# A float32 transformer trunk on one core: the first pair of hidden chunks of each half step by eight plain block products of 512 columns

## The chip, the cores and the metric

The program runs on one core of a Trainium2 chip. The time is the device time of one execution in microseconds (us); lower is better. A core has TensorE (PE in the profile; its weight loads are PEld), VectorE (DVE), ScalarE (ACT), GpSimd (POOL) and SyncE (SP, here the issuer of the weight DMAs). Each engine takes its instructions from a list of its own, in the order of that list, and waits at an instruction until what it needs is there.

## The reference

Two layers on 512 tokens of width 1024, in float32. Each layer has two half steps (a gated feed-forward net of hidden width 2816), a token mixer between them and a gated embedding at the end:

```python
def rms_norm(x, g, eps=NORM_EPS):
    x32 = x.astype(f32)
    y = x32 * lax.rsqrt(jnp.mean(x32 * x32, axis=-1, keepdims=True) + eps)
    return (y * g.astype(f32)).astype(x.dtype)

def swiglu(h, wg, wu, wd):
    return (jax.nn.silu(h @ wg) * (h @ wu)) @ wd
...
    for i in range(DEPTH):
        h = h + 0.5 * swiglu(rms_norm(h, norm_ffn_a[i]), ffn_a_wg[i], ffn_a_wu[i], ffn_a_wd[i])
        hn = rms_norm(h, norm_mix[i])
        ...
        h = h + mix
        h = h + 0.5 * swiglu(rms_norm(h, norm_ffn_b[i]), ffn_b_wg[i], ffn_b_wu[i], ffn_b_wd[i])
        gate = jax.nn.sigmoid(rms_norm(h, norm_ple[i]) @ ple_gate[i])
        h = h + gate * (p[i] @ ple_proj[i])
    return rms_norm(h, final_norm)
```

The mixers are left out here; the change does not touch them.

## The kernel before

The state is kept transposed: `hT[c]` holds 128 of the 1024 channels (c = 0 to 7) for all 512 tokens. A float32 factor is split into a high part (rounded to fp32r, a copy on ACT) and a low part (the rest, a subtraction on DVE), and a product is three matmuls: high by high, high by low, low by high (`mm3`). The normalization is not applied to the operand. Only the gain is; the reciprocal root mean square R of each token is worked out from the running sum of squares `acc` by `norm_stats` (four matmuls `ssum`, eleven tiny DVE instructions, a diagonal matrix L336, a matmul `rbc` that spreads it over the partitions, a copy L345 into `Rt`) and multiplied in after the product.

A half step (`ffn`) runs through 22 hidden chunks of 128 in sections of 4, 6, 6 and 6 (`SECTIONS`). Chunks are taken in pairs j (`dq`, `pair`): for a pair, gate and up projection are 1024 by 512 by 512 products, cut into a two by two scheme (channel blocks in even and odd c, tokens in two halves of 256, the two chunks) and done by **seven** block products instead of eight. Each `product` is 24 matmuls of 256 columns (2 for gate and up, 4 channel blocks, 3 for the split). The seven need sums of weights, which `split_next` adds up on DVE (L165) before it splits them (L174 on ACT, L176 on DVE), seven pieces for a pair; and sums of operands, `xr`, seven combinations of the activations. `right(i)` makes those of channels 2i and 2i+1: two scalings on ACT (L366, L368), four sums of 256 columns on DVE (L377 to L380), and the split of seven blocks (L373 on ACT, L374 on DVE, in parts of 3 and 4). Op 0 is needed by the first product (tile X), op 3 by the second (tile Y), and both need all four i. Between the pairs stand the down projections of the section before (`down`, 512 columns each).

There are four half-step starts. In the two of `fa` in layer 0 (the launch) and of `fb` in both layers, `prep` calls `right` after every second channel block becomes final: at the launch after a transposition (L440), in `fb` after the last output projection of the mixer (`out_proj`, the add L772). In `fa` of layer 1 it happens inside the gated embedding `ple` (L553 to L556), where `prep(..., part=True)` makes most of the sums, and `rest` (L386 to L390) the two blocks that `ple` does not leave free; `ple_x` is the operand of `ple`.

The order of the instructions on each engine is set at build time by a scheduler that plays the program through; the program's order gives priority. Weights come through six raw buffers (`load_next`) into five split slots (`hl`); a slot is free again when the product that reads it is done (`used`, `pump`). Each of the PSUM tags A (X), B (Y) and C (Z) has two banks.

Of the kernel before, what the change touches and what calls it, by code (L numbers as in the profile page):

```python
# [18 lines left out]
P = 128  # L19
# [19 lines left out]
def trunk(ctx, tc, a, stop=None):  # L39
# [7 lines left out]
    def bank(tag, name="ps"):  # L47
        return psum.tile([P, NT], F32, tag=tag, name=name)
# [172 lines left out]
    def plan_ffn(wg, wu, wd):  # L221


        base = [sum(SECTIONS[:s]) for s in range(len(SECTIONS))]
        steps = []

        def dq(j):
            q = {}
            for f, par in ((0, 0), (1, 0), (1, 1), (0, 1)):
                cs = slice((2 * j + f) * P, (2 * j + f + 1) * P)  # L230
                dmas = [(lambda t, u=u: t.rearrange("p (i n) -> p i n", i=4)[:, :, u * P : (u + 1) * P],
                         w[:, cs].rearrange("(i two p) n -> p two i n", two=2, p=P)[:, par])
                        for u, w in enumerate((wg, wu))]
                q[f, par] = Raw(1024, dmas, True)
            a, b, c, d = q[0, 0], q[0, 1], q[1, 0], q[1, 1]
            steps.append(("dq", j, [
                Piece(1024, a), Piece(1024, None, (0, c, d)), Piece(1024, None, (0, 0, a)),
                Piece(1024, None, (0, 0, b)), Piece(1024, None, (1, a, c)), Piece(1024, b),
                Piece(1024, d)]))

        def dn(s, u):
            n = SECTIONS[s]
            rows = slice(base[s] * P, (base[s] + n) * P)
            steps.append(("dn", s, u, Unit(n, 256, [(0, n, 0, wd[rows, u * 256 : (u + 1) * 256])], True)))

        for s, n in enumerate(SECTIONS):
            us = list(range(4)) if s else []
            js = [base[s] // 2 + k for k in range(n // 2)]
            for k, j in enumerate(js):
                dq(j)  # L250
                for _ in range(len(us) // (len(js) - k)):
                    dn(s - 1, us.pop(0))
        for u in range(4):
            dn(len(SECTIONS) - 1, u)
        return steps
# [88 lines left out]
        else:  # L344
            nc.vector.tensor_copy(dst, ps)  # L345

    def prep(c, l, which, sq=True, eng=nc.vector, part=False):


        g = gains[:, l, which, c : c + 1]  # L350
        if which % 2:
            h, lw = ple_x[c] if which == 3 else (xh[c], xl[c])
            nc.scalar.activation(h, hT[c], AF.Copy, scale=g)
            nc.vector.scalar_tensor_tensor(lw, hT[c], g, h.bitcast(F32),
                                           op0=ALU.mult, op1=ALU.subtract)
        elif c % 2:
            right(c // 2, l, which, part)
        if sq:
            squares(c, eng)

    ple_x = [(hid[4 + 2 * c], hid[5 + 2 * c]) for c in range(4)]
    ple_x += [tuple(xrt[:, s, 1024 + c * NT : 1536 + c * NT] for s in range(2)) for c in range(4)]

    def right(i, l, which, part=False):
# [6 lines left out]
        def halve(o, v, n):  # L371
            h, lw, s = xr[:, 0, o : o + n, i, :], xr[:, 1, o : o + n, i, :], V[:, v : v + n]
            nc.scalar.activation(h, s, AF.Copy)  # L373
            nc.vector.tensor_tensor(lw, s, h.bitcast(F32), op=ALU.subtract)  # L374
# [9 lines left out]
    def rest(i, l, which):  # L384

        g = gains[:, l, which, 2 * i + 1 : 2 * i + 2]  # L386
        h, lw = (xr[:, s, 1:3, i, :] for s in range(2))
        x = hT[2 * i + 1].rearrange("p (o n) -> p o n", o=2)
        nc.scalar.activation(h, x, AF.Copy, scale=g)
        nc.vector.scalar_tensor_tensor(lw, x, g, h.bitcast(F32), op0=ALU.mult, op1=ALU.subtract)  # L390

    def squares(c, eng=nc.vector):
        if c == 0:
# [51 lines left out]
    pump()  # L445


    def ffn(steps, nxt, side=None):

        state = {}  # L450

        def pair(j, ps, first):
            X, Y, Z = bank("A", "X"), bank("B", "Y"), bank("C", "Z")
            k = [0]

# [88 lines left out]
    def ple(pt, ids, R, nxt):  # L544

        for c in range(KD):
            pg, pj = bank("A", "pg"), bank("B", "pj")
            for k in range(2):
                mm3(pj, *ids[c].w(8 + k), *pt[k], k == 0, k == 1)
            for k in range(KD):  # L550
                mm3(pg, *ids[c].w(k), *ple_x[k], k == 0, k == KD - 1)
            s = sc("sg")
            nc.vector.tensor_tensor(s, pg, R, op=ALU.mult)  # L553
            nc.scalar.activation(s, s, AF.Sigmoid)
            nc.vector.tensor_tensor(s, pj, s, op=ALU.mult)
            nc.vector.tensor_tensor(hT[c], s, hT[c], op=ALU.add)  # L556
            done(ids[c])
            prep(c, *nxt, part=True)
        for i in range(4):
            rest(i, *nxt)  # L560

    def last_ple(pt, d, rcol):

# [12 lines left out]
        for i, iu in enumerate(d["pg"]):  # L576
            for b in range(NB):
                ts_ = slice(b * P, (b + 1) * P)
                ps = bank("A", "pg")
                for k in range(KD):  # L580
                    mm3(ps, ple_x[k][0][:, ts_], ple_x[k][1][:, ts_], *iu[k // 4].w(k % 4),
                        k == 0, k == KD - 1)
                ph = bank("D", "hps")
                for c in range(4):
# [482 lines left out]


    for l, d in enumerate(plans):
        ffn(d["fa"], (l, 1))  # L1070
        rcol, _ = norm_stats(False)
        (odd_mixer if l else even_mixer)(d, rcol, (l, 2))
        box = []
        ffn(d["fb"], (l, 3), lambda: box.append(load_p(l)))
# [44 lines left out]
```

## Time and profile before

| | |
|---|---|
| three runs | 2177.76, 2178.45, 2184.96 us; median 2178.45 us |
| profiled execution, its own time | 2182.95 us |
| its span | 2181.2 us |
| PE busy | 2059.2 us (94%), 13283 matmuls |
| DVE busy | 1696.4 us (78%) |
| ACT busy | 1068.1 us (49%) |
| POOL busy | 281.1 us (13%) |
| mean granted clock of TensorE | 0.966 |
| DMA | 190.06 MB, mean 87 GB/s |

The span is that of one profiled execution, cut by its own clock; the few us between span and time lie around it. PE's share is an average. In nearly all of the 40 slices of the page PE is busy for nine tenths or more; the first slice and the few at the starts of half steps are not, and there the granted clock is lower too (0.6 in the first slice). So what a change at a half-step start is worth is read from the stretch from the first final channel block to the point from which PE runs without a gap.

### The profile page before, as it was taken

What the parts mean: (1) busy time and instruction counts of PE and PEld (TensorE: products, weight loads), DVE (VectorE), ACT (ScalarE), POOL (GpSimd) and SP (SyncE); (2) the same over time, 40 slices, a digit from 0 to 9 for tenths busy, and PEclk for the clock granted to TensorE, in tenths of its full rate; (3) what the DMA queues carried; (4) which work ended last, traced back from release to release, by engine and by line L of the source; (5) the groups of instructions that cost most, each with busy time, mean ns of one, the idle gap of its engine ahead of it and who ended that gap; (6) DMA issues with size and microseconds to landing.
All of it is one profiled execution on the core that took longest, in us unless ns stands there. A gap on an engine that the chain in (4) does not pass through costs nothing.

```text
span 2181.2 us, 34325 instructions
## 1 busy us (share of the span) xinstructions
PE 2059.2 (94%) x13283; PEld 1885.6 (86%) x13283; DVE 1696.4 (78%) x2682; ACT 1068.1 (49%) x1722; POOL 281.1 (13%) x249
## 2 busy tenths in 40 slices
PE   4999999999788899999999999999999879999998
PEld 3999998988766799999779999989989769999986
DVE  7888777688988897786788877767656689877775
ACT  4544444355555554444555444445655555444443
POOL 2000000433411000000410000014323110000011
PEclk6999999998899899999999999999999979999999
DMA  4333333321111233333333333222212214333331
GB/s 130 107 110 96 92 97 100 78 61 48 60 39 39 73 102 107 112 105 93 86 90 107 102 102 116 88 80 78 69 44 75 78 39 122 98 95 103 114 109 39
DMA packets 302051, 190.06 MB, mean 87 GB/s; under 512 B 14208, under 2 KB 292800, under 8 KB 301888
## 3 DMA queue, kind: packets, MB, share of 16 engines
q1 hardware_dynamic: 298592, 184.36, 28.6%
q10 hardware_dynamic: 2912, 2.46, 0.4%
q8 instruction: 104, 1.70, 0.3%
q0 software_dynamic: 384, 1.05, 0.2%
q14 instruction: 59, 0.48, 0.1%
HBM read 185.73 MB, written 2.10 MB: 86 GB/s over the span
## 4 chain that ended last, share of the span: by engine, by line
PE 84%; DVE 12%; issue 1%; ACT 1%; DMA 1%; SPq 0%; POOL 0%; DVEq 0%; ACTq 0%; POOLq 0%
PE X L464 22%; PE Y L464 11%; PE down L310 7%; PE down L309 7%; PE down L308 7%; PE Z L464 6%; PE proj L308 3%; PE proj L309 3%; PE proj L310 3%; DVE fr L165 1%; DVE xr L374 1%; PE outp L309 1%; PE outp L308 1%; PE outp L310 1%; PE pt L717 1%
## 5 line engine op out<-in xcount | busy, mean ns | idle before, releaser
L174 ACT ACTIVATE hl<-fr 128x1024 fp32r<-128x1024 f32 (+5 forms) x620 | 522.2, 860 | 662.2 <-PE X L464 285.0
L176 DVE TENSOR_TENSOR hl<-fr,hl 128x1024 fp32r<-128x1024 f32 (+2 forms) x485 | 548.0, 1137 | 155.8 <-ACT hl L174 150.2
L464 PE MATMUL X<-xr,hl 128*128 128x256 f32 x4224 | 539.5, 284 | 27.4 <-DVE xr L374 24.5
L464 PEld LDWEIGHTS X<-xr,hl 128*128 128x128 f32 x4224 | 522.4, 191 | 39.4 <-DVE xr L374 28.6
L464 PE MATMUL Y<-xr,hl 128*128 128x256 f32 x2112 | 274.2, 285 | 19.8 <-ACT xr L373 11.2
L464 PEld LDWEIGHTS Y<-xr,hl 128*128 128x128 f32 x2112 | 259.9, 191 | 26.5 <-ACT xr L373 12.5
L310 PE MATMUL down<-hid,hl 128*128 128x512 f32 x704 | 274.2, 390 | 0.0
L308 PE MATMUL down<-hid,hl 128*128 128x512 f32 x704 | 274.2, 390 | 0.0
L309 PE MATMUL down<-hid,hl 128*128 128x512 f32 x704 | 274.2, 389 | 0.0
L165 DVE TENSOR_TENSOR fr<-fr 128x1024 f32<-128x1024 f32 x176 | 218.6, 1242 | 24.7 <-DMA fr<-in_ffn_b_wu_dram 11.5
L176 POOL TENSOR_TENSOR hl<-fr,hl 128x512 fp32r<-128x512 f32 (+3 forms) x135 | 155.8, 1172 | 271.5 <-ACT hl L174 205.8
L308 PE MATMUL proj<-hl,xr 128*128 128x384 f32 (+2 forms) x512 | 170.4, 336 | 5.4 <-DVE fr L633 4.1
L309 PE MATMUL proj<-hl,xr 128*128 128x384 f32 (+2 forms) x512 | 170.2, 333 | 0.0
L310 PE MATMUL proj<-hl,xr 128*128 128x384 f32 (+2 forms) x512 | 169.7, 333 | 0.0
L310 PEld LDWEIGHTS down<-hid,hl 128*128 128x128 f32 x704 | 132.2, 188 | 26.3
L308 PEld LDWEIGHTS down<-hid,hl 128*128 128x128 f32 x704 | 132.2, 188 | 25.1
L309 PEld LDWEIGHTS down<-hid,hl 128*128 128x128 f32 x704 | 132.2, 188 | 24.6
L464 PE MATMUL Z<-xr,hl 128*128 128x256 f32 x1056 | 147.9, 284 | 2.7 <-DVE hl L176 1.7
L464 PEld LDWEIGHTS Z<-xr,hl 128*128 128x128 f32 x1056 | 135.3, 192 | 3.1 <-DVE hl L176 1.9
L641 POOL TENSOR_TENSOR fr<-fr 128x512 f32<-128x512 f32 (+1 forms) x72 | 90.6, 1265 | 219.2 <-DVE fr L633 109.8
L308 PEld LDWEIGHTS proj<-hl,xr 128*128 128x128 f32 x512 | 98.0, 192 | 7.4 <-DVE fr L633 4.3
L513 DVE TENSOR_TENSOR fr<-down,fr 128x512 f32<-128x512 f32 x128 | 87.6, 684 | 20.3 <-PE down L310 19.4
(211 smaller groups left out, 2920.3 us busy)
## 6 DMA issues: line engine op xcount, KB each, us to landing
fr<-in_ffn_a_wg_dram SPq DMA_DIRECT2D x88, 256.0 KB, 2.9
fr<-in_ffn_a_wu_dram SPq DMA_DIRECT2D x88, 256.0 KB, 3.3
fr<-in_ffn_b_wg_dram SPq DMA_DIRECT2D x88, 256.0 KB, 2.9
fr<-in_ffn_b_wu_dram SPq DMA_DIRECT2D x88, 256.0 KB, 3.3
fr<-in_ffn_a_wd_dram SPq DMA_DIRECT2D x48, 384.0 KB, 3.7
fr<-in_ffn_b_wd_dram SPq DMA_DIRECT2D x48, 384.0 KB, 3.8
fr<-in_odd_w_in_dram SPq DMA_DIRECT2D x96, 128.0 KB, 2.5
fr<-in_even_w_in_dram SPq DMA_DIRECT2D x56, 128.0 KB, 2.8
```

The source lines that it names most:

```text
L165: nc.vector.tensor_tensor(src, *(sums[x] if isinstance(x, int) else x.ap() for x in (a, b)), op=ALU.add)
L174: nc.scalar.activation(hi[:, s:e], src[:, s:e], AF.Copy)
L176: eng.tensor_tensor(lo[:, s:e], src[:, s:e], hi[:, s:e].bitcast(F32), op=ALU.subtract)
L308: nc.tensor.matmul(ps, lh, rh, start=first, stop=False)
L309: nc.tensor.matmul(ps, lh, rl, start=False, stop=False)
L310: nc.tensor.matmul(ps, ll, rh, start=False, stop=last)
L374: nc.vector.tensor_tensor(lw, s, h.bitcast(F32), op=ALU.subtract)
L464: nc.tensor.matmul(o, w[lw][:, i, us], xr[:, r, op, i, :], start=start and u == 0 and i == 0 and n == 0, stop=i == 3 and n == 2, skip_grou ...
L513: nc.vector.tensor_tensor(t, ps, state["R"], op=ALU.mult)
L641: nc.gpsimd.tensor_tensor(dst, rv, tv, op=ALU.add)
L717: nc.tensor.transpose(ps[:, off : off + P], es[b][:, c * P : (c + 1) * P], ident)
```

## The change

The pair j = 0 of each half step is no longer done by seven products of sums, but by the eight plain block products (`plain`): for each of the two chunks f, gate (tile G, tag A) and up (tile U, tag B) are 8 channel blocks times 3 matmuls of 512 columns, 96 matmuls for the pair in place of 168 of 256 columns. It needs four weight pieces, no weight sums, and as operand only the plain split of each channel block (`plain_x`: even c in `hid`, odd c in ops 1 and 2 of `xr`, where the scheme of seven wants that block as well). `prep` makes just this split, L357 on ACT and L358 on DVE. The operand sums (`right`) follow in the program after the first 48 matmuls and after the second 48, so they can be made while those run; op 0 is now a negated copy on ACT (L369), and one split of four blocks is left (L381, L382). R is worked out after the first 48. Then come the outputs of the two chunks (L459 to L463). `part` and `rest` are gone; `ple` and the last embedding read the ordinary operand `xh`, `xl` (ops 3 to 6 of `xr`).

```diff
-            for f, par in ((0, 0), (1, 0), (1, 1), (0, 1)):
+            for f, par in ((0, 0), (1, 0), (1, 1), (0, 1)) if j else ((0, 0), (0, 1), (1, 0), (1, 1)):
...
+            if j == 0:
+                steps.append(("pl", [Piece(1024, r) for r in (a, b, c, d)]))
+                return
...
+        h, lw = (xh[c], xl[c]) if which % 2 else plain_x[c]
+        x = hT[c]
+        if not which % 2 and c % 2:
+            x = x.rearrange("p (o n) -> p o n", o=2)
+        nc.scalar.activation(h, x, AF.Copy, scale=g)
+        nc.vector.scalar_tensor_tensor(lw, x, g, h.bitcast(F32), op0=ALU.mult, op1=ALU.subtract)
...
+    plain_x = [(hid[12 + c], hid[13 + c]) if c % 2 == 0 else
+               tuple(xr[:, s, 1:3, c // 2, :] for s in range(2)) for c in range(KD)]
...
+        nc.scalar.activation(xr[:, 0:2, 0, i, :], hidt[:, 12 + 2 * i : 14 + 2 * i, 256:], AF.Copy,
+                             scale=-1.0)
...
-        halve(0, 1, 1 if part else 3)
-        halve(3, 4, 4)
...
+        h, lw = xr[:, 0, 3:7, i, :], xr[:, 1, 3:7, i, :]
+        nc.scalar.activation(h, V[:, 4:8], AF.Copy)
+        nc.vector.tensor_tensor(lw, V[:, 4:8], h.bitcast(F32), op=ALU.subtract)
...
+        def plain(ps):
+            for f in range(2):
+                G, U = bank("A", "G"), bank("B", "U")
+                for c in range(KD):
+                    w = [ps[2 * f + c % 2].part(s).rearrange("p (i n) -> p i n", i=4)[:, c // 2, :]
+                         for s in range(2)]
+                    for u, t in enumerate((G, U)):
+                        us = slice(u * P, (u + 1) * P)
+                        mm3(t, w[0][:, us], w[1][:, us], *plain_x[c], c == 0, c == KD - 1)
+                used(*ps[2 * f : 2 * f + 2])
+                if f == 0:
+                    state["R"] = norm_stats()[1]
+                for i in (2 * f, 2 * f + 1):
+                    right(i, *me)
+                g, u = (O[:, 1, k, :] for k in range(2)) if f else aeb[:2]
+                nc.vector.tensor_tensor(g, G, state["R"], op=ALU.mult)
+                nc.scalar.activation(g, g, AF.Silu)
+                nc.vector.tensor_tensor(u, U, g, op=ALU.mult)
+                nc.scalar.activation(hid[f], u, AF.Copy)
+                nc.vector.tensor_tensor(hid[6 + f], u, hid[f].bitcast(F32), op=ALU.subtract)
...
-            if first:
-                state["R"] = norm_stats()[1]
...
-            prep(c, *nxt, part=True)
-        for i in range(4):
-            rest(i, *nxt)
+            prep(c, *nxt)
```

How the change moves instructions is shown at the start of `fb` in layer 0. First TensorE's list before, where the statistics end and the first products run in full (X, Y and Z are the tiles of pair 0; the numbers tell tiles of one name apart):

```order
L464 MATMUL X_6330<-xr_79,hl_81 128x256 x15
L341 MATMUL rbc_6411<-fr_82,ones_69 128x512
L464 MATMUL Y_6331<-xr_79,hl_81 128x256 x15
L464 MATMUL Z_6332<-xr_79,hl_81 128x256 x2
L464 MATMUL X_6330<-xr_79,hl_81 128x256 x24
L464 MATMUL Z_6332<-xr_79,hl_81 128x256 x8
L464 MATMUL Y_6331<-xr_79,hl_81 128x256 x24
```

The same place in the change: G and U are the plain tiles of the second chunk, X, Y and Z those of pair 1.

```order
L312 MATMUL G_6337<-xr_79,hl_81 128x512
L313 MATMUL G_6337<-xr_79,hl_81 128x512
L312 MATMUL U_6338<-xr_79,hl_81 128x512
L313 MATMUL U_6338<-xr_79,hl_81 128x512
L329 MATMUL ssum_6292<-ones_69,fr_82 128x1 x4
L344 MATMUL rbc_6311<-fr_82,ones_69 128x512
L477 MATMUL X_6420<-xr_79,hl_81 128x256 x24
L477 MATMUL Y_6421<-xr_79,hl_81 128x256 x24
L477 MATMUL Z_6422<-xr_79,hl_81 128x256 x2
```

The statistics' two groups of matmuls, which stood among the products of pair 0, now stand behind all 96 plain matmuls and ahead of every product of pair 1.

VectorE's list before, at the end of the statistics (L336) and of the operand sums (L374):

```order
L321 SCALAR_TENSOR_TENSOR rcol_6391<-rq_6398,rcol_6391 128x4
L374 TENSOR_TENSOR xr_79<-fr_82,xr_79 128x3x256
L378 TENSOR_TENSOR fr_82<-fr_82 128x256
L336 TENSOR_TENSOR fr_82<-ident_64,rcol_6391 128x512
L380 TENSOR_TENSOR fr_82<-fr_82 128x256
L374 TENSOR_TENSOR xr_79<-fr_82,xr_79 128x4x256
L176 TENSOR_TENSOR hl_81<-fr_82,hl_81 128x1024
L345 COPY fr_82<-rbc_6411 128x512
L176 TENSOR_TENSOR hl_81<-fr_82,hl_81 128x1024 x2
L486 TENSOR_TENSOR fr_82<-Y_6331,fr_82 128x2x256
```

And in the change, at the end of the statistics (L339) and the first reads of G and U (L459, L461):

```order
L176 TENSOR_TENSOR hl_81<-fr_82,hl_81 128x1024
L323 SCALAR_TENSOR_TENSOR rq_6298<-rq_6298,rv_6297 128x4
L165 TENSOR_TENSOR fr_82<-fr_82 128x1024
L324 SCALAR_TENSOR_TENSOR rcol_6291<-rq_6298,rcol_6291 128x4
L339 TENSOR_TENSOR fr_82<-ident_64,rcol_6291 128x512
L348 COPY fr_82<-rbc_6311 128x512
L459 TENSOR_TENSOR fr_82<-G_6235,fr_82 128x512
L459 TENSOR_TENSOR fr_82<-G_6337,fr_82 128x512
L461 TENSOR_TENSOR fr_82<-U_6236,fr_82 128x512
L461 TENSOR_TENSOR fr_82<-U_6338,fr_82 128x512
```

The last operand sums (L382) now stand some rows ahead of this place, weight splits and sums of pair 1 (L176, L165) have moved in among the tiny instructions of the statistics, and the reads of G and U follow on them at once.

## Rows read from the trace of the kernel before

**Rows 1.** Waits of TensorE, the longest entry: us in total, times, longest us.
```profile
PE X L464 <- DVE xr L374: 24.5, 11, 4.5
```

**Rows 2.** Stretches at the starts: length, busy PE, PEld, DVE, ACT, POOL; PEclk, DMA, GB/s.
```profile
14.36:52.86 38.50, 17.04 (x58) 12.30 (x57) 36.79 (x51) 18.94 (x24) 12.44 (x7) 0.52 0.27 80
693.49:728.55 35.06, 18.78 (x61) 13.34 (x62) 32.07 (x52) 20.00 (x27) 7.48 (x5) 0.64 0.05 15
723.00:729.00 6.00, 5.28 (x20) 4.28 (x20) 4.17 (x9) 2.40 (x3) 0.00 (x0) 0.50 0.00 0
1122.22:1146.95 24.73, 20.07 (x132) 18.68 (x130) 20.42 (x36) 11.71 (x17) 0.00 (x0) 0.86 0.21 62
1744.12:1778.81 34.69, 18.42 (x62) 13.24 (x62) 32.08 (x52) 19.63 (x27) 7.49 (x5) 0.66 0.05 16
```

**Rows 3.** VectorE in order of time: start us, us, what, start of `fb`, layer 0.
```profile
693.49 1.28 DVE L772 TENSOR_TENSOR h<-outp,h 128x512 f32<-128x512 f32 x2
...
706.90 2.29 DVE L374 TENSOR_TENSOR xr<-fr,xr 128x1024 fp32r<-128x1024 f32 x1
...
709.71 1.21 DVE L176 TENSOR_TENSOR hl<-fr,hl 128x1024 fp32r<-128x1024 f32 x1
710.84 0.41 DVE L377 TENSOR_TENSOR fr<-fr 128x256 f32<-128x256 f32 x1
...
712.99 1.21 DVE L165 TENSOR_TENSOR fr<-fr 128x1024 f32<-128x1024 f32 x1
...
720.64 0.16 DVE L319 TENSOR_TENSOR rq<-rcol 128x4 f32<-128x4 f32 x1
720.84 0.16 DVE L320 SCALAR_TENSOR_TENSOR rq<-rq,rv 128x4 f32<-128x4 f32 x1
...
726.82 1.22 DVE L374 TENSOR_TENSOR xr<-fr,xr 128x1024 fp32r<-128x1024 f32 x1 [1.12 <-ACT xr L373]
```

**Rows 4.** VectorE, the same view, elsewhere: launch, `ple`, start of `fb` in layer 1.
```profile
12.41 0.68 DVE L440 COPY h<-xps 128x512 f32<-128x512 f32 x1
...
1126.56 0.74 DVE L390 SCALAR_TENSOR_TENSOR xr<-h,gains,xr 128x512 fp32r<-128x512 f32 x1
...
1744.12 1.28 DVE L772 TENSOR_TENSOR h<-outp,h 128x512 f32<-128x512 f32 x2
```

**Rows 5.** TensorE in order of time, at the four starts.
```profile
74.40 0.40 PE L464 MATMUL Z<-xr,hl 128*128 128x256 f32 x2
...
724.48 3.35 PE L464 MATMUL X<-xr,hl 128*128 128x256 f32 x14 [0.72 <-DVE xr L374]
...
727.63 1.91 PE L341 MATMUL rbc<-fr,ones 128*128 128x512 f32 x2
...
731.85 2.88 PE L464 MATMUL X<-xr,hl 128*128 128x256 f32 x24
...
747.94 2.88 PE L464 MATMUL Y<-xr,hl 128*128 128x256 f32 x24
750.66 0.39 PE L464 MATMUL Z<-xr,hl 128*128 128x256 f32 x2
...
1122.22 1.20 PE L464 MATMUL X<-xr,hl 128*128 128x256 f32 x9
...
1158.26 2.99 PE L464 MATMUL X<-xr,hl 128*128 128x256 f32 x24
...
1799.96 0.39 PE L464 MATMUL Z<-xr,hl 128*128 128x256 f32 x2
```

**Rows 6.** TensorE, matmuls of 512 columns, down projection.
```profile
335.05 0.39 PE L310 MATMUL down<-hid,hl 128*128 128x512 f32 x1
335.27 0.39 PE L308 MATMUL down<-hid,hl 128*128 128x512 f32 x1
```

**Rows 7.** TensorE, matmuls of 512 columns, mixer's last output projection, layer 1.
```profile
1756.52 0.63 PE L309 MATMUL outp<-hid,hl 128*128 128x512 f32 x1
1756.95 0.63 PE L310 MATMUL outp<-hid,hl 128*128 128x512 f32 x1
```

More of the change, by code (lines that the diff above doesn't have):

```diff
@@ L345, in spread, with prep, right @@
             nc.vector.tensor_copy(dst, ps)
-    def prep(c, l, which, sq=True, eng=nc.vector, part=False):
+    def prep(c, l, which, sq=True, eng=nc.vector):
         g = gains[:, l, which, c : c + 1]
[L351 to L357, printed above, removed]
+        h, lw = (xh[c], xl[c]) if which % 2 else plain_x[c]
[4 more added lines that the diff above has]
+        nc.vector.scalar_tensor_tensor(lw, x, g, h.bitcast(F32), op0=ALU.mult, op1=ALU.subtract)
         if sq:
             squares(c, eng)
-    ple_x = [(hid[4 + 2 * c], hid[5 + 2 * c]) for c in range(4)]
-    ple_x += [tuple(xrt[:, s, 1024 + c * NT : 1536 + c * NT] for s in range(2)) for c in range(4)]
-    def right(i, l, which, part=False):
+    plain_x = [(hid[12 + c], hid[13 + c]) if c % 2 == 0 else
+               tuple(xr[:, s, 1:3, c // 2, :] for s in range(2)) for c in range(KD)]
+    def right(i, l, which):
+        nc.scalar.activation(xr[:, 0:2, 0, i, :], hidt[:, 12 + 2 * i : 14 + 2 * i, 256:], AF.Copy,
+                             scale=-1.0)
         nc.scalar.activation(V[:, 0:2].rearrange("p s n -> p (s n)"), hT[2 * i], AF.Copy,
@@ L369, in right @@
                              scale=gains[:, l, which, 2 * i + 1 : 2 * i + 2])
[L371 to L374, printed above, removed]
         v = nc.vector
@@ L380, in right @@
         v.tensor_tensor(V[:, 7], V[:, 3], V[:, 5], op=ALU.subtract)
-        halve(0, 1, 1 if part else 3)
-        halve(3, 4, 4)
[L384 to L390, printed above, removed]
+        h, lw = xr[:, 0, 3:7, i, :], xr[:, 1, 3:7, i, :]
+        nc.scalar.activation(h, V[:, 4:8], AF.Copy)
+        nc.vector.tensor_tensor(lw, V[:, 4:8], h.bitcast(F32), op=ALU.subtract)
     def squares(c, eng=nc.vector):
@@ L445, in trunk, with ffn, pair @@
     pump()
-    def ffn(steps, nxt, side=None):
+    def ffn(steps, me, nxt, side=None):
         state = {}
-        def pair(j, ps, first):
+        def plain(ps):
[18 more added lines that the diff above has]
+                nc.vector.tensor_tensor(hid[6 + f], u, hid[f].bitcast(F32), op=ALU.subtract)
+        def pair(j, ps):
             X, Y, Z = bank("A", "X"), bank("B", "Y"), bank("C", "Z")
@@ L520, in ffn @@
         for k, st in enumerate(steps):
-            if st[0] == "dq":
-                pair(st[1], st[2], k == 0)
+            if st[0] == "pl":
+                plain(st[1])
+            elif st[0] == "dq":
+                pair(st[1], st[2])
             else:
@@ L550, in ple @@
             for k in range(KD):
-                mm3(pg, *ids[c].w(k), *ple_x[k], k == 0, k == KD - 1)
+                mm3(pg, *ids[c].w(k), xh[k], xl[k], k == 0, k == KD - 1)
             s = sc("sg")
@@ L580, in last_ple @@
                 for k in range(KD):
-                    mm3(ps, ple_x[k][0][:, ts_], ple_x[k][1][:, ts_], *iu[k // 4].w(k % 4),
+                    mm3(ps, xh[k][:, ts_], xl[k][:, ts_], *iu[k // 4].w(k % 4),
                         k == 0, k == KD - 1)
@@ L1069, in trunk @@
     for l, d in enumerate(plans):
-        ffn(d["fa"], (l, 1))
+        ffn(d["fa"], (l, 0), (l, 1))
         rcol, _ = norm_stats(False)
@@ L1073, in trunk @@
         box = []
-        ffn(d["fb"], (l, 3), lambda: box.append(load_p(l)))
+        ffn(d["fb"], (l, 2), (l, 3), lambda: box.append(load_p(l)))
         if l == 0:
```

## The prediction

> **What bounds the kernel now.** I read the page first, then TensorE's waits, then the windows of the four half-step starts, then VectorE and TensorE there in order of time. On the page TensorE is busy 94% of the span; it is without work for any length only at the starts. Its longest entry of waits says so: product X waits for the low part of the operand, L374 on VectorE, 24.5 us in 11 waits [rows 1]. In the windows the reader is to see who is full: from the first final channel block of `fb` in layer 0, 35.06 us, VectorE is busy 32.07 and TensorE 18.78, at a granted clock of 0.64; at the launch 36.79 of 38.50 against 17.04, in layer 1 32.08 of 34.69 against 18.42. Only in `fa` of layer 1 are the two alike (20.42 and 20.07 of 24.73) [rows 2]. So a start is as long as VectorE's list, and TensorE has slack. I call the starts S1 (launch), S2 (`fb`, layer 0), S3 (`fa`, layer 1) and S4 (`fb`, layer 1). From the end of tile Y of pair 1 the same matmuls follow in both kernels, without a gap; that point (74.40, 750.66, 1158.26, 1799.96 [rows 5]) is where I compare.
>
> **The change, part by part.** *Prices on VectorE.* The next instruction begins about 0.08 us before the one ahead of it has ended (L176, 1.21 long, at 709.71, the next at 710.84), so each counts from start to start: an add or copy of 512 columns 0.60 (two in 1.28), a sum of 256 columns 0.34, a split of 1024 columns 1.13 (L176, L165, and the split of four blocks L382 taken alike), a tiny one 0.20 (720.64 to 720.84) [rows 3]. The plain split L358 has the form of L390, 0.74 long, 0.66 to the next [rows 4]. While POOL runs one of its adds, VectorE's instruction beside it is longer: L374 took 2.29 instead of 1.22 [rows 3]. I count 1.07 for each POOL add; there are 5 in S2 and S4, 7 at the launch [rows 2], and the change keeps them.
>
> *The new path.* The statistics stand behind the plain matmuls, and tile X of pair 1 stands behind the statistics: G of both chunks fills the two banks of tag A, so X waits for L459, L459 for Rt (L348), that for `rbc` and L339. What was hidden among the products of pair 0 now ends the start. So I add up VectorE's list to L339, as the order of the changed kernel has it. S2, from 693.49: 8 adds 4.8, 8 L358 5.3, 16 sums 5.4, 4 L382 4.5, 2 adds of squares 1.2, 6 L176 6.8, 5 L165 5.7, 11 tiny ones 2.2, L339 0.6: 36.5, and 5 POOL adds 5.4, together 41.9. The kernel before, added up alike to 728.05, is 33.2 where the trace has 34.6, so 1.3 is to be added for waits: L339 ends at 736.7. Then `rbc` 1.9 (1.91 at 727.63 [rows 5]), the copy L348 0.6, L459 0.7 and 0.4 between engines, 3.6 in all: X at 740.3. S4 has the same list: 1744.12 [rows 4] plus 43.2 plus 3.6 is 1790.9. S1, from 12.41 [rows 4]: 6 copies 3.6, one more of that size 0.6, 8 L358 5.3, 16 sums 5.4, 3 L382 3.4, 8 L176 9.0, 6 L165 6.8, tiny ones and L339 2.8: 36.9, with 7 POOL adds 7.5, 44.4, and 1.1 for waits: 57.9, X at 61.5. S3, from 1122.22, where `ple` leaves TensorE [rows 5]: the list there to L459, which covers `rbc` with weight splits, is 25.3; 1.1 more for the split L381, which must wait until `ple` has read the blocks that it overwrites, and 2.2 for the row sums, which stand behind the plain matmuls: X at 1150.8.
>
> *TensorE.* A matmul of 512 columns takes 0.225 (335.05 to 335.27 [rows 6]) and one of 256 at the same level 2.72/24 = 0.113 (747.94 to 750.66 [rows 5]). So the pair costs 96 x 0.225 = 21.6 instead of 168 x 0.113 = 19.0: 2.6 more, four times, which the slack at the starts hides; without it this is 10.4 against the change. In S2 the last channel block is split about 25 us into the list (718.5); behind it stand 12 matmuls, 2.7, and the row sums 1.9: done at 723.1, before VectorE comes to read them. So TensorE then waits some 13 us for L339 and again for L459.
>
> *X and Y.* At which level do X and Y run after that? The clock is 0.50 from 723 to 729 (the lower level, 1.2 GHz) [rows 2], after a stretch in which TensorE had mostly waited; there 14 matmuls take 3.15 (724.48 to 727.63), 0.225 each, and from about 732 on the products have the short time again [rows 5]. I take X of S1, S2 and S4 at the lower level (24 x 0.225 = 5.4) and Y at the upper (2.7; 2.8 in `fa`). In S3 TensorE has worked densely and waits 4 us only, at a mean of 0.86 there [rows 2]: 2.8 or 5.4, I take 4.1.
>
> So Y ends at 61.5 + 8.2 = 69.7 in S1 (gain 4.7), 748.4 in S2 (2.3), 1157.7 in S3 (0.6), 1799.0 in S4 (1.0). The sum is 8.6 us.
>
> The Trainium skill says in "TensorE: Matmul & The Clock Gate", section "Loop structure matters more than you think", that the loop nest decides whether the array stays warm and that a long wait between matmuls makes them run cold. It speaks against this change, which puts a wait of 13 us ahead of X; that the clock is 0.50 at 723 after waiting agrees with it. By that rule alone, with Y cold as well, the time is that of rival (c), 2182; by the rows above it is 2169.8.
>
> *Edits at nothing.* `ple` and the last embedding read another place of the same size; TensorE is full there, and VectorE has no more to do there than before. The weight DMAs are as many, the fourth piece (d) in another place of the queue, and no piece is waited for at the starts. The weight sums saved (three of 1024 columns a pair) are in the lists above. If VectorE were no longer the later one in `ple`, nothing would change; if a weight piece came late, it costs the wait, up to 2 us a start. Of what the trace of before does not show I bound: waits on VectorE's new list, 2 us less or more a start (the two corrections, 1.1 and 1.3, are nearest, so I take these); X's level, 2.7 each.
>
> **Rivals.**
> (a) *X and Y at the upper level throughout.* For it: the waits are short against what is asked of TensorE, 96 long matmuls ahead of them in a stretch that held 61 of all kinds before [rows 2]. Against it: 0.50 at 723. Gain 8.6 + 3 x 2.7 + 1.3 = 18.0: 2160.5.
> (b) *The list on VectorE is held up twice more a start.* ACT splits first, and weight slots come free only when the plain matmuls have read them; a wait of this kind was 1.12 at 726.82 [rows 3]. Two of them make 2.2 a start, 8.8 in all: no change, 2178.7. Against it: VectorE has other work queued at most places.
> (c) *X and Y both at the lower level after the wait.* Y then takes 5.4 too, 2.7 more four times, and X of S3 1.3 more: 12.1 against 8.6, 2182. Against it: the products are short again from 731.85 on [rows 5], 7 us after the dense work at the lower level began; since X alone is 5.4, a part of Y may still be long.
> (d) *Slower: the plain matmuls themselves run at the lower level.* There 512 columns take 0.43 (1756.52 to 1756.95 [rows 7]). From 696.5 the 96 of S2 then end at 737.8, with the row sums 739.7, and behind the first tiny instruction that reads them stand 11 us of VectorE's list, tiny ones, weight splits and L339: 750.7, 14 later than I have it. At 0.38 on average this is 9.4 later in S2 and S4, 5.5 at the launch: 8.6 - 24.3 = 15.7 slower, 2194; at 0.43 throughout about 2207. It decides from about 0.33 on, where the delays eat the gain. For it: clocks of 0.52, 0.64, 0.66 at these starts [rows 2]. Against it: at 0.43 the stream would be busy without a gap, while the low clocks of before belong to a TensorE busy for half of the stretch.
> (e) *The sums are not made during the plain products.* By the order, only about half of them stand ahead of the last channel block; the rest runs when TensorE is done. That is in the lists already and costs no more.
>
> **How the numbers follow.** The profiled execution takes 2182.95 by its own time (span 2181.2), 4.5 above the median 2178.45; with 8.6 less it is 2174.35, and the median 2169.8. The forecast has 0.48, with its own range of 2164.5 to 2175; (a) 0.18, (b) 0.13, (c) 0.07, (d) 0.14; (e) is no case apart. I count 0.3%, 6.5 us, as what can be told from no change: faster is below 2171.9, slower above 2185. Of the forecast 0.38 lies below 2171.9 and 0.10 above: faster 0.38 + 0.18 = 0.56, same 0.10 + 0.13 + 0.07 = 0.30, slower 0.14. The range 2159 to 2184 takes in all but (d) and the edge of (a).
>
> **What would show it.** In the profile after: a wait of TensorE at X for L459, four times, 10 to 14 us with `rbc` in it at S1, S2 and S4 and about 4 at S3; the last plain matmul at S2 near 721 and L339 ending near 737, counted on this time scale; X of 24 matmuls in about 5.4 and Y in about 2.7; plain matmuls at 0.225 (rival (d) if above 0.33); VectorE full up to L459. Wrong would be a Y of pair 1 that ends later than before at S1 or S2, a gap on TensorE after Y that was not there, or a clock that stays at 0.50 through Y.

## The result and the profile after

| | before | changed |
|---|---|---|
| runs | 2177.76 to 2184.96 us, median 2181.23 (4) | 2162.31 to 2164.67 us, median 2164.26 (4) |
| ratio | | 0.992, 95% interval 0.9899 to 0.9942 |
| span of the profiled execution | 2181.2 us | 2162.5 us |
| PE busy | 2059.2 us, 13283 matmuls | 2048.6 us, 12995 matmuls |
| DVE busy | 1696.4 us | 1663.7 us |

The change makes the kernel faster by 0.8% (0.6 to 1.0%), some 17 us; 8.6 were forecast. The time lies in the range that was given, and the direction is the one forecast; the size is twice the forecast. So two questions follow: whether the starts do what the prediction says, and where the other half comes from.

TensorE's longest waits in the changed kernel (us in total, times, longest) are these; X's wait for L374 [rows 1] is gone:

```profile
PE rbc L344 <- DVE fr L339: 38.0, 4, 13.6
PE X L477 <- DVE fr L459: 8.3, 4, 3.6
```

The new wait is the one that was foreseen, in two parts, at each of the four starts: `rbc` waits for L339, and X then for L459. In the windows of the starts (length, busy PE, PEld, DVE, ACT, POOL; granted clock) the first and third line are the plain products of the launch and of `fb` in layer 0, the line behind each the wait up to X, and the two after that X and Y of `fb` in layer 0; the last is X of `fb` in layer 1:

```profile
12.30:41.86 29.56, 28.71 (x120) 22.38 (x120) 28.37 (x35) 21.52 (x33) 11.91 (x7) 0.88 0.55 161
41.86:59.25 17.39, 2.22 (x4) 0.54 (x3) 16.16 (x31) 7.41 (x9) 0.00 (x0) 0.64 0.21 61
688.60:718.26 29.66, 27.79 (x122) 22.08 (x122) 29.17 (x39) 22.46 (x34) 7.07 (x5) 1.00 0.19 54
718.26:733.66 15.40, 2.08 (x3) 0.51 (x3) 12.93 (x27) 4.55 (x6) 0.00 (x0) 0.64 0.23 69
733.66:738.95 5.29, 5.29 (x25) 5.29 (x26) 3.25 (x5) 2.50 (x4) 0.00 (x0) 0.50 0.00 0
738.95:742.05 3.10, 3.10 (x25) 3.10 (x25) 1.22 (x1) 1.55 (x2) 0.00 (x0) 0.88 0.00 0
1774.39:1778.62 4.23, 4.23 (x24) 4.23 (x25) 3.26 (x5) 2.50 (x4) 0.00 (x0) 0.65 0.01 4
```

The reader is to see three things against [rows 2]. The plain products fill TensorE (27.79 of 29.66 us) and run at a clock of 0.88 and 1.00, where the stretch had 0.52 and 0.64 before. Then, for 15 to 17 us, TensorE has nothing but `rbc` to do (2.08 and 2.22 us) while VectorE works on. And X after that runs at 0.50 to 0.65, Y already at 0.88. TensorE in order of time, at the launch, `fb` of layer 0, `fa` of layer 1 and `fb` of layer 1, answers to [rows 5]:

```profile
55.60 2.05 PE L344 MATMUL rbc<-fr,ones 128*128 128x512 f32 x2 [13.56 <-DVE fr L339]
64.23 2.88 PE L477 MATMUL Y<-xr,hl 128*128 128x256 f32 x24
66.95 0.39 PE L477 MATMUL Z<-xr,hl 128*128 128x256 f32 x2
730.07 2.08 PE L344 MATMUL rbc<-fr,ones 128*128 128x512 f32 x2 [11.81 <-DVE fr L339]
733.66 5.49 PE L477 MATMUL X<-xr,hl 128*128 128x256 f32 x24 [1.51 <-DVE fr L459]
742.05 0.39 PE L477 MATMUL Z<-xr,hl 128*128 128x256 f32 x2
1141.98 4.62 PE L477 MATMUL X<-xr,hl 128*128 128x256 f32 x24 [3.65 <-DVE fr L459]
1149.26 0.40 PE L477 MATMUL Z<-xr,hl 128*128 128x256 f32 x2
1774.39 4.39 PE L477 MATMUL X<-xr,hl 128*128 128x256 f32 x24 [1.51 <-DVE fr L459]
1781.34 0.39 PE L477 MATMUL Z<-xr,hl 128*128 128x256 f32 x2
```

The end of Y of pair 1, which is the start of Z, lies 7.45, 8.61, 9.00 and 18.62 us earlier than before (74.40, 750.66, 1158.26 and 1799.96 in [rows 5]). The same instructions elsewhere in the two traces show where these sums grow. A start of `fb` is counted as the prediction counts it, from the first add of a final channel block (693.49 and 1744.12 before [rows 3, 4]; 688.60 and 1729.34 now) to the end of Y. Between the launch and the mixer another 1.17 come in, and the two mixers change the sums too:

| stretch | gain in the two traces, us | forecast, us |
|---|---|---|
| launch, to Y of pair 1 | 7.45 | 4.7 |
| from there to the first down projection (105.49 before, 96.87 after) | 1.17 | 0 |
| from there to the first final block of layer 0, the mixer above all | -3.73 | 0 |
| start of `fb`, layer 0 | 3.72 | 2.3 |
| from there to the end of `ple` (1122.22 before, 1114.18 after) | -0.57 | 0 |
| start of `fa`, layer 1 | 0.96 | 0.6 |
| from there to the first final block of layer 1, the mixer above all | 5.78 | 0 |
| start of `fb`, layer 1 | 3.84 | 1.0 |

The rows sum to 18.62. The four starts give 16.0 where 8.6 were forecast, and the two mixers, in which the change edits nothing, move by -3.73 and 5.78. In the mixer of layer 1 the trace of before shows this on VectorE and, behind it, on TensorE (the last line is a window):

```profile
1707.81 1.23 DVE L165 TENSOR_TENSOR fr<-fr 128x1024 f32<-128x1024 f32 x1 [2.67 <-DMA fr<-in_ffn_b_wu_dram]
1709.07 0.43 DVE L662 TENSOR_TENSOR hid<-qkps,hid 64x256 fp32r<-64x256 f32 x1
1709.55 0.44 PE L670 MATMUL qk<-hid 128*128 128x384 f32 x1 [3.37 <-DVE hid L662]
1709.55:1725.00 15.45, 13.94 (x60) 11.17 (x61) 10.40 (x28) 9.92 (x25) 0.00 (x0) 0.78 0.12 35
```

and the changed kernel this at the same place:

```profile
1697.50 0.43 DVE L673 TENSOR_TENSOR hid<-qkps,hid 64x256 fp32r<-64x256 f32 x1 [1.35 <-ACT hid L670]
1697.98 0.44 PE L681 MATMUL qk<-hid 128*128 128x384 f32 x1 [0.80 <-DVE hid L673]
1697.98:1709.00 11.02, 10.61 (x56) 8.35 (x57) 8.96 (x26) 9.35 (x24) 0.00 (x0) 1.00 0.17 51
```

Before, a weight sum (L165) of the coming `fb` stood in VectorE's list ahead of the copies L662 of the attention and waited 2.67 us for its weight; TensorE waited 3.37 us for L662 and afterwards ran for a while at a clock of 0.78 on average. The plain pair has no weight sums, so nothing of this stands at that place now, and up to a matmul a little later (1729.08 before, 1713.12 now) 6.96 us are gained. But the sums have not gone from the mixers: the first is now one of pair 1, 8 us ahead of the first final block where the old one came 36 us ahead. The same place of layer 0 before, and then layer 0 and layer 1 of the changed kernel:

```profile
682.36 1.21 DVE L165 TENSOR_TENSOR fr<-fr 128x1024 f32<-128x1024 f32 x1
684.22 0.50 PE L308 MATMUL outp<-hid,hl 128*128 128x512 f32 x1 [0.22 <-DVE h L772]
```

```profile
678.95 1.22 DVE L165 TENSOR_TENSOR fr<-fr 128x1024 f32<-128x1024 f32 x1 [2.90 <-DMA fr<-in_ffn_b_wu_dram]
680.83 0.50 PE L311 MATMUL outp<-hid,hl 128*128 128x512 f32 x1 [2.12 <-DVE h L783]
681.63:685.27 3.64, 3.64 (x10) 2.83 (x9) 0.69 (x1) 0.00 (x0) 0.00 (x0) 0.53 0.02 5
1721.28 1.23 DVE L165 TENSOR_TENSOR fr<-fr 128x1024 f32<-128x1024 f32 x1 [1.91 <-DMA fr<-in_ffn_b_wu_dram]
1723.16 0.50 PE L311 MATMUL outp<-hid,hl 128*128 128x512 f32 x1 [1.13 <-DVE h L783]
1729.34 0.69 DVE L783 TENSOR_TENSOR h<-outp,h 128x512 f32<-128x512 f32 x1
```

In layer 0, where no sum waited in the mixer before, TensorE now waits 2.12 us behind one and runs on at a clock of 0.53: the gain falls there from 7.97 to 4.89 us. In layer 1 it falls from 15.96 to 14.78. Not all of the -3.73 is the change's: in the traces of three kernels below whose layer 0 is as before (the change at `fb` of layer 1 alone, at the launch alone, and the sums on POOL), the stretch up to the first final block of layer 0 is itself 1.1 to 2.9 us longer than in the trace of before.

### The profile page after: what moved, and what is told of

The parts are those of the page before. It is cut to its first block, busy times and chain, and to the rows that moved or that the text cites. A ratio compares the mean times of both kernels' runs of the same rounds, so it can differ in the third digit from the quotient of the medians.

```text
span 2162.5 us, 33689 instructions
## 1 busy us (share of the span) xinstructions
PE 2048.6 (95%) x12995; PEld 1865.1 (86%) x12995; DVE 1663.7 (77%) x2666; ACT 1061.6 (49%) x1730; POOL 277.0 (13%) x249
## 4 chain that ended last, share of the span: by engine, by line
PE 84%; DVE 12%; issue 2%; DMA 1%; ACT 1%; SPq 0%; DVEq 0%; POOL 0%; ACTq 0%
PE X L477 21%; PE Y L477 10%; PE down L313 7%; PE down L311 7%; PE down L312 7%; PE Z L477 5%; PE proj L311 3%; PE proj L312 3%; PE proj L313 3%; PE pg L311 1%; PE pg L312 1%; PE pg L313 1%; PE pt L728 1%; PE outp L311 1%; PE outp L312 1%
## 5 line engine op out<-in xcount | busy, mean ns | idle before, releaser
L174 ACT ACTIVATE hl<-fr 128x1024 fp32r<-128x1024 f32 (+4 forms) x608 | 509.0, 856 | 651.6 <-PE X L477 285.3
L176 DVE TENSOR_TENSOR hl<-fr,hl 128x1024 fp32r<-128x1024 f32 (+2 forms) x473 | 530.0, 1128 | 164.6 <-ACT hl L174 161.1
L477 PE MATMUL X<-xr,hl 128*128 128x256 f32 x3840 | 484.8, 283 | 8.3 <-DVE fr L459 8.3
L477 PEld LDWEIGHTS X<-xr,hl 128*128 128x128 f32 x3840 | 474.7, 192 | 19.7 <-DVE fr L459 10.6
L477 PE MATMUL Y<-xr,hl 128*128 128x256 f32 x1920 | 238.3, 281 | 0.0
L477 PEld LDWEIGHTS Y<-xr,hl 128*128 128x128 f32 x1920 | 231.1, 189 | 0.0
L165 DVE TENSOR_TENSOR fr<-fr 128x1024 f32<-128x1024 f32 x160 | 197.8, 1237 | 25.4 <-DMA fr<-in_ffn_b_wu_dram 13.2
L176 POOL TENSOR_TENSOR hl<-fr,hl 128x512 fp32r<-128x512 f32 (+3 forms) x135 | 153.5, 1154 | 275.0 <-ACT hl L174 202.0
L477 PE MATMUL Z<-xr,hl 128*128 128x256 f32 x960 | 132.7, 280 | 0.0
L477 PEld LDWEIGHTS Z<-xr,hl 128*128 128x128 f32 x960 | 121.3, 189 | 0.0
```

What stands on the lines that cost most here:

```text
L165: nc.vector.tensor_tensor(src, *(sums[x] if isinstance(x, int) else x.ap() for x in (a, b)), op=ALU.add)
L174: nc.scalar.activation(hi[:, s:e], src[:, s:e], AF.Copy)
L176: eng.tensor_tensor(lo[:, s:e], src[:, s:e], hi[:, s:e].bitcast(F32), op=ALU.subtract)
L477: nc.tensor.matmul(o, w[lw][:, i, us], xr[:, r, op, i, :], start=start and u == 0 and i == 0 and n == 0, stop=i == 3 and n == 2, skip_grou ...
```

## The experiments

All ratios are to the kernel before, with their 95% intervals; "us less" is the ratio applied to 2182.9 us, the median of before in these runs. The change by that measure is 17.5 us less.

**Does the mixer's gain come from the weight sum?** In the kernel before, the first two weight sums of that pair go to POOL:

```diff
+            eng = nc.gpsimd if getattr(p, "pool", False) else nc.vector
-            nc.vector.tensor_tensor(src, ...)
+            eng.tensor_tensor(src, ...)
...
+    for p in plans[1]["fb"][0][2][1:3]:
+        p.pool = True
```

> The kernel before, with two of the four weight sums of pair 0 of fb in layer 1 (sum of c and d, and that plus a) on POOL instead of VectorE. Theory (7 us of the change's gain come from the mixer of layer 1, where such a sum stands on VectorE ahead of the copies L662 and waits 2.67 us for its DMA, and TensorE waits 3.37 us and then runs at the lower clock): the wait at L662 is under 1 us, the clock stays at 1.00 and the time falls by 5 to 7 us, ratio 0.997 to 0.998. Rival (the gain in that mixer comes from the new order of TensorE's or ACT's list): no change, ratio 0.9995 to 1.001.

Measured: 0.9973 (0.9963 to 0.9984), 5.9 us less. TensorE's wait at the place is now 0.79 us and the clock of the stretch 1.00 (the lines are TensorE's and a window's):

```profile
1710.06 0.44 PE L671 MATMUL qk<-hid 128*128 128x384 f32 x1 [0.79 <-DVE hid L663]
1708.00:1724.00 16.00, 13.67 (x78) 10.77 (x77) 11.51 (x31) 11.73 (x30) 3.60 (x2) 1.00 0.35 101
```

The rival (a new order of TensorE's or ACT's list) would have shown no change. So the sum on VectorE's list was the cause: without anything else of the change, moving it off VectorE gives 5.9 us, 3.5 to 8.1 by the interval. The traces say the same: from the first down projection of `fa` to the first final block, layer 1 is 5.7 us shorter in this run than in the kernel before and 5.6 to 6.0 shorter in all nine kernels with the plain pair at `fb` of layer 1, while with the change at the launch alone it is 0.5 longer.

**One start at a time.** Kernels with the change at some starts only (the plain pair, its split and its operand sums there, the old way elsewhere). `PLAIN` names the starts by layer and half step, 0 for `fa` and 2 for `fb`:

```diff
+    PLAIN = {(1, 2)}
...
+            if pl and j == 0:
+                steps.append(("pl", [Piece(1024, r) for r in (a, b, c, d)]))
+                return
...
+        elif (l, which) in PLAIN:
+            h, lw = plain_x[c]
```

At `fb` of layer 1 alone:

> The kernel before, with the change at the start of fb in layer 1 alone (plain products there, the rest as before). Theory (there the change gives 7 us in the mixer ahead of the start, where no weight sum stands on VectorE any more, and 2.7 at the start itself): 8 to 10.5 us less than the kernel before, ratio 0.9952 to 0.9964. Rival (only the start counts, and the mixer's gain comes from elsewhere in the change): 1 to 3 us, ratio 0.9986 to 0.9996.

Measured: 0.9955 (0.9943 to 0.9968), 9.8 us less, as the mixer and the start together had in the traces (5.78 + 3.84). At the launch alone:

> The kernel before, with the change at the launch alone. Theory (the launch's start is shorter by itself: Y of pair 1 ends 7.4 us earlier, and 1.2 more come from the shorter period of the matmuls behind it): 7 to 9 us less than the kernel before, ratio 0.9958 to 0.9968. By the prediction's own term it would be 4.7 us, 0.9978. Rival (the launch's gain depends on how the other starts are done): outside 4 to 10 us.

Measured: 0.9981 (0.9972 to 0.9990), 4.1 us less. That is the prediction's 4.7, not the 7 to 9 that the theory expected from the 8.6 of the traces, though this kernel's own profiled execution shows 8.55 at the first down projection too. Its ten runs lie between 2174.32 and 2182.11 us, and the profiled one is the fastest of them. In the traces the launch itself is steady where it is plain: the first down projection starts at 96.87 to 96.94 in this kernel, the changed one and the one with all starts but `fa`; in the four with the old launch it starts at 103.43 to 106.86. So the stretch is 6.5 us shorter at the least, while 2.2 to 6.1 by the interval is what the kernel's times show. Where the other executions give the rest back no trace shows. At both starts of `fb`, and at all but `fa` of layer 1:

> The kernel before, with the change at the two starts of fb alone. By the prediction's terms the start of fb in layer 0 gives 2.3 us, so with the 10.1 us that fb of layer 1 gave alone it is 12.4, ratio 0.9943. Theory (from the trace of the changed kernel, where the start of fb in layer 0 gains about 0.6 us and the mixer ahead of it nothing): 10.7 us, 0.9951. Rival (a gain in the mixer of layer 0 as in that of layer 1): over 15 us, below 0.993.

> The kernel before, with the change at the launch and at both starts of fb, and the old way at fa of layer 1. Theory (starts add up: 4.2 us timed or 8.6 in the profile at the launch, 10.1 and 0.6 to 2.3 at fb): 15 to 20 us less than the kernel before, ratio 0.991 to 0.993, the same as the changed kernel, as the start of fa in layer 1 gives nothing (0.6 by the prediction). Rival (that start carries a part of the gain of 17 us): below 13 us, ratio 0.994 or above.

Measured: 0.9927 (0.9914 to 0.9940), 15.9 us less, and 0.9906 (0.9891 to 0.9921), 20.5 us less. The first misses both numbers (12.4 and 10.7) and just meets the rival's condition (over 15 us, below 0.993), a gain in the mixer of layer 0 too. With 9.8 taken off for layer 1, `fb` of layer 0 and its mixer give about 6 (2 to 10 by the two intervals), where the prediction had 2.3 and the trace of the changed kernel none. That the mixer gives it is not shown: from the first down projection to the first final block of layer 0 the trace of this run gains 1.2 us, that of all but `fa` loses 1.5, that of the changed kernel 3.7. The start behind that point is steadier: up to the first down projection it is 3.7 to 4.0 us shorter in the three. The second run fits the sum of the parts (4.1 + 15.9 = 20.0). It can't be told from the full change (the intervals overlap; 3 us less by the ratios), so `fa` of layer 1 shows no gain in the times, and whether it costs something is open.

**Does X wait only because G holds the banks of tag A?** The plain tiles of the second chunk go to tag C:

```diff
-                G, U = bank("A", "G"), bank("B", "U")
+                G, U = bank("C" if f else "A", "G"), bank("C" if f else "B", "U")
```

> The changed kernel, with the plain tiles of the second chunk (G and U of f = 1) in the two banks of tag C, so that X and Y of pair 1 have a free bank of tags A and B and need not wait for R. Theory (X waits for the statistics only because G holds both banks of tag A): X no longer waits for L459 but starts right after the fourth operand split L382, at the start of fb in layer 0 about 8 us earlier against the plain matmuls; Z takes the wait for L459. Y of pair 1 and the point where TensorE runs on without a gap come 4 to 6 us earlier at three starts and 2 to 3 at fa of layer 1: 14 to 20 us less than the changed kernel, ratio to the kernel before 0.983 to 0.986. Rival (VectorE's list as a whole bounds the start, whichever wait ends it): Z waits as long as X did, gain under 3 us, ratio 0.991 to 0.992.

Measured: 0.9846 (0.9827 to 0.9864), 33.6 us less than before and 16 less than the change. TensorE at `fb` of layer 0:

```profile
716.79 2.89 PE L477 MATMUL X<-xr,hl 128*128 128x256 f32 x24
722.68 2.49 PE L477 MATMUL Y<-xr,hl 128*128 128x256 f32 x14 [1.86 <-DVE xr L382]
728.40 2.07 PE L344 MATMUL rbc<-fr,ones 128*128 128x512 f32 x2 [3.23 <-DVE fr L339]
732.67 5.19 PE L477 MATMUL Z<-xr,hl 128*128 128x256 f32 x24 [2.20 <-ACT fr L460]
```

X starts without a wait, Y waits 1.86 us for the operand split L382, and now Z is the first that has to wait for R, and runs at the lower level in X's place. The theory holds: the wait that the change adds is a matter of two PSUM banks.

**Is X slow because TensorE stood still?** Matmuls of no use fill the wait:

```diff
+                if f:
+                    D, t = bank("C", "warm"), xr[:, 1, 3:5, 2, :]
+                    for k in range({(1, 0): 24, (0, 0): 42}.get(me, 50)):
+                        nc.tensor.matmul(D, t[:, 0, :P], t, start=True, stop=True)
```

> The changed kernel, with 42, 50, 24 and 50 extra matmuls of 512 columns (of no use, into a bank of tag C that nobody reads) at the four starts, between the plain matmuls and X, so that TensorE does not idle while the statistics are made. Theory (X runs slowly because TensorE idled before it): the granted clock stays at 1.00 and X's 24 matmuls take 2.7 to 2.8 us instead of 5.0, 5.3, 4.5 and 4.2; 5 to 8 us less than the changed kernel in all, ratio 0.988 to 0.990. If the short period of 0.113 us of a 256-column matmul after a start comes from the rest before it, it is gone as well and X starts the products at 0.118. Rival (X is slow for another reason, such as its first weights): X as slow as before, no gain or up to 2 us loss, ratio 0.992 to 0.993.

Measured: 0.9886 (0.9871 to 0.9902), 7.4 us less than the change. The two intervals just touch, but each of its four times (2154.35 to 2159.41 us) is below each of the change's. TensorE at `fb` of layer 0, and the window of X:

```profile
715.59 11.64 PE L461 MATMUL warm<-xr 128*128 128x512 f32 x50
727.53 1.12 PE L344 MATMUL rbc<-fr,ones 128*128 128x512 f32 x2 [0.31 <-DVE fr L339]
730.17 3.01 PE L481 MATMUL X<-xr,hl 128*128 128x256 f32 x24 [1.51 <-DVE fr L463]
730.17:733.01 2.84, 2.84 (x24) 2.84 (x25) 2.69 (x5) 2.51 (x4) 0.00 (x0) 1.00 0.02 6
```

With 50 matmuls more, X takes 2.84 us in place of 5.29, at a clock of 1.00. The Trainium skill ("TensorE: Matmul & The Clock Gate", section "Loop structure matters more than you think") says that the loop nest decides whether matmuls stay warm, and that they run cold behind a long wait (its example waits for a DMA). This run agrees with it: X behind the wait ran at 0.50, X behind the filled wait at 1.00.

**Is it VectorE's list that makes L339 late?** Two ways to shorten what stands ahead of it. One Newton step in place of three at the four starts (R is then less exact; the run is for its time):

```diff
-        for _ in range(3):
+        for _ in range(1 if pw else 3):
...
-                    state["R"] = norm_stats()[1]
+                    state["R"] = norm_stats(pw=True)[1]
```

> The changed kernel, with one Newton step instead of three in the statistics of the four starts (five tiny instructions instead of eleven; R is less exact, this run is for its time alone). The list of VectorE between the first tiny instruction and L339 then has 8, 11, 10 and 11 instructions instead of 24, 19, 18 and 19; at the start of fb two weight operations of 1.13 and six tiny ones go from it, 3.5 us. Theory (X waits for L339, and L339 for what VectorE's list puts ahead of it): X starts 3 to 4 us earlier at both starts of fb, 2 at fa of layer 1, 3 to 8 at the launch, where the last split L382 then comes behind L339; 11 to 17 us less than the changed kernel, ratio to the kernel before 0.985 to 0.988. Rival (X needs something else by then, such as the operand split L382 or its first weights): less than 4 us, ratio 0.991 or above.

Measured: 0.9856 (0.9842 to 0.9869), 14.0 us less than the change. At `fb` of layer 0 X comes 42.0 us behind the first final block, and 45.1 in the change. The other way, the Newton steps as twelve instructions on POOL:

```diff
+            if e is nc.gpsimd:
+                e.tensor_tensor(q, q, v, op=ALU.mult)
+                e.tensor_scalar(q, q, -0.5, 1.5, op0=ALU.mult, op1=ALU.add)
+                e.tensor_tensor(dst, dst, q, op=ALU.mult)
+                continue
...
-                    state["R"] = norm_stats()[1]
+                    state["R"] = norm_stats(e=nc.gpsimd)[1]
```

> The changed kernel, with nine of the eleven tiny instructions of the four starts' statistics (the three Newton steps) on POOL, as twelve instructions, instead of VectorE. Theory (X waits for L339, and L339 for its place in VectorE's list): nine tiny ones of 0.20 and one or two weight splits go from ahead of L339, X starts 2 to 4 us earlier at three starts; 6 to 10 us less than the changed kernel, ratio 0.987 to 0.989. Rival (POOL's chain of twelve takes longer than VectorE's list did, or the clock takes the gain back): no gain, ratio 0.991 or above.

Measured: 0.9922 (0.9908 to 0.9936), no gain, as the rival has it. POOL and VectorE (the split L387 is L382 of the change, L344 its L339) at `fb` of layer 0:

```profile
720.71 4.51 POOL L322 TENSOR_TENSOR rq<-rcol 128x4 f32<-128x4 f32 x1 [15.72 <-DVE rcol L319]
725.30 0.20 POOL L324 TENSOR_TENSOR rq<-rq,rv 128x4 f32<-128x4 f32 x1
...
723.95 1.22 DVE L165 TENSOR_TENSOR fr<-fr 128x1024 f32<-128x1024 f32 x1
728.32 0.69 DVE L344 TENSOR_TENSOR fr<-ident,rcol 128x512 f32<-128x512 f32 x1 [3.16 <-POOL rcol L326]
```

VectorE's list did become shorter, and VectorE then waited 3.16 us for POOL. POOL's first tiny instruction lasted 4.51 us and ended when VectorE's row of large ones did (725.22 and 725.17); the next took only 0.20.

**Both together.** The spare banks with two Newton steps:

```diff
+                G, U = bank("C" if f else "A", "G"), bank("C" if f else "B", "U")
...
+        for _ in range(2 if pw else 3):
```

> The changed kernel with the second chunk's plain tiles in tag C (as in the run with the spare banks) and two Newton steps instead of three in the statistics of the four starts. Theory (with X and Y out of the way, Z still waits for L339): L339 comes 0.6 us earlier by the three tiny ones and another 1 to 4 us where weight splits leave its list, so Z starts 1 to 4 us earlier at each start; 2 to 8 us less than with the spare banks alone, ratio to the kernel before 0.981 to 0.984. Rival (Z then waits for weights, or for ACT at L460): no further gain, 0.9845.

Measured: 0.9840 (0.9826 to 0.9853), 2147.44 us. L339 and Z come about two us earlier at `fb` of layer 0 (Z at 730.48 after 732.67), but by the times it can't be told from the spare banks alone. The spare banks are the version to take: they change one line, keep R as it was, and are faster than the kernel before and the changed one.

## Why the prediction was right, and what it missed

**The path at the starts: right.** The end of VectorE's list was named as what X would wait for, and it is. The list at `fb` of layer 0, from the first final block to the end of the path:

```profile
688.60 0.68 DVE L783 TENSOR_TENSOR h<-outp,h 128x512 f32<-128x512 f32 x1
...
723.25 1.22 DVE L382 TENSOR_TENSOR xr<-fr,xr 128x1024 fp32r<-128x1024 f32 x1
...
729.32 0.69 DVE L339 TENSOR_TENSOR fr<-ident,rcol 128x512 f32<-128x512 f32 x1
732.18 0.69 DVE L348 COPY fr<-rbc 128x512 f32<-128x512 f32 x1 [2.17 <-PE rbc L344]
732.91 1.29 DVE L459 TENSOR_TENSOR fr<-G,fr 128x512 f32<-128x512 f32 x2
```

From 688.60 to the end of L339 (730.01) are 41.4 us, where 41.9 and 1.3 for waits were forecast; from there to X are 3.7 us, forecast 3.6. At `fa` of layer 1 the way from the end of `ple` (1114.18) to X is 27.8, forecast 28.6; at the launch X came at 59.25, forecast 61.5. The run with the shorter statistics shows that it is the list, and the one with the spare banks that it is the two banks. Rival (b), two more waits on the list, is not seen: VectorE's waits of more than 0.2 us up to L339 are one of 1.12 at the launch, one of 0.46 here, and 0.59 and 0.46 at `fb` of layer 1.

**TensorE's extra work at nothing: right.** The 96 plain matmuls ran at 0.23 us and were done when VectorE came to read the row sums; the extra 24 to 50 matmuls of the warm run at each start, up to 11.6 us of TensorE, cost nothing either.

**The levels of X and Y: right in the main.** X took 4.98, 5.29 and 4.23 us where 5.4 was forecast and 4.45 at `fa` where it was 4.1, Y 2.72 to 3.10 (2.7). So X of `fb` in layer 1, at a clock of 0.65, ran a good part of the way at the upper level. Rival (a), both at the upper level, was worked out at 9.4 us more; the warm run, which makes it true, gives 7.4. Rival (c) would have Y at 5.4, and rival (d) a plain matmul over 0.33 us; neither is seen.

**The missing half, first: the list was added up too long.** From the first final block (at `fa` from the end of `ple`) to the end of Y the four starts were forecast at 57.3, 54.9, 35.5 and 54.9 us and measure 54.65, 53.45, 35.08 and 52.00, 7.4 us less in all. For 6.4 of them X comes earlier than the sum has it: by 2.1, 1.8, 0.8 and 1.7. At `fb` of layer 0 the sum to L339 is 1.8 too long, and three terms were too high: waits 0.5 and not 1.3, POOL's adds 4.6 and not 5.4, and the eleven tiny instructions 1.7 and not 2.2 (the other rows take 0.3 more). A tiny one took 0.20 where the next needs its result (725.71 to 725.91), and 0.07 to 0.12 where it does not (719.30 to 719.37). The error is on one side at all four starts, and the price of the statistics' path, called right above, is right in its mechanism and too high in its size.

**The missing half, second: the term for the weight sums.** Under "Edits at nothing" the prediction said that the weight sums saved, three a pair, are in the lists above. There are four a pair (seven pieces, three of them plain), and that they are in the lists was the step that failed. The lists begin at the first final block; but the sums for the first pair of `fb` are made from weights that come earlier, so VectorE meets some of them inside the mixer, and there one stood ahead of a copy for which TensorE waits. The row was in the trace of before (VectorE at 1707.81, a wait of 2.67 us for a DMA, and TensorE's 3.37 behind it), outside the windows that were read. It measures 5.78 in the table, and 5.9 by the run that moves two sums to POOL. The term has the other sign too: in layer 0 a sum of pair 1 now waits where none did, and TensorE 2.12 us behind it.

In the traces the 18.62 are thus 8.6 as forecast, 7.4 for the lists and for X, 2.05 for the two mixers together and 0.6 for the stretches between. In the times this split is not settled. By times `fb` of layer 0 with its mixer gives about 6, the launch 4 and `fa` of layer 1 nothing or a loss; by the trace of the changed kernel these parts are 0.0, 8.6 and 1.0. Stretches that are alike in two kernels differ by 2 us in single traces (the unchanged launch of the kernel with both `fb` starts is 2.06 earlier than before), so a term of that size can't be read from one.

## What to carry to other kernels

When an operand's preparation is removed, look for all the places where its instructions stood, not only at the step that uses it: on an engine that works through a list in order, an early instruction that waits for a DMA holds up everything behind it. A result that is needed late (here R) may still hold banks that the next step needs early; count the buffers on the way before a step is moved. Here a spare bank was worth as much as a shorter chain (33.6 and 31.4 us less than before, the intervals overlap) and left R as it was. And here a wait of TensorE cost twice: once itself, and once in what ran slowly after it (X 5.29 us instead of 2.84). Last, when several gaps are priced from one list, read the price of a row off rows of the same kind: a tiny instruction with an independent one behind it, a POOL add, a wait.

## What the runs showed of the hardware

A POOL instruction of four columns lasted 4.51 us beside back-to-back instructions of VectorE with 1024 columns (5.65 at the launch, 4.51 at `fb` of layer 1), and 0.20 us without. In [rows 3] it is the other way round: there VectorE's L374 is the one that takes 2.29 instead of 1.22 us.

At a granted clock of 1.00 the matmuls of 256 columns have two periods, 0.113 and 0.118 us. A product of 24 matmuls shortly after the launch, from its start to the next one's, in the kernel before (pair 0, 2.82 us) and in the changed one (pair 1, 2.72 us):

```profile
61.68 2.99 PE L464 MATMUL X<-xr,hl 128*128 128x256 f32 x24
64.50 1.58 PE L464 MATMUL Z<-xr,hl 128*128 128x256 f32 x12
```

```profile
67.18 2.88 PE L477 MATMUL X<-xr,hl 128*128 128x256 f32 x24
69.90 1.07 PE L477 MATMUL Z<-xr,hl 128*128 128x256 f32 x8
```

In the changed kernel the shorter period lasts until the first down projections have run (the X at 101.42 and that at 776.52 have 0.118 again), and it makes the 1.17 us between Y and the first of them. It does not come from TensorE's rest ahead of it: in the warm run it is there without the rest, at `fa` of layer 1 even where the changed kernel has 0.118. Its cause stays open.
